# Ranking the weight split of the spilled expert blocks ahead of the list decode in a two-layer encoder step

## The chip, the cores and the metric

The kernel runs on one core of one Trainium2 chip. The metric is device time of one execution in microseconds (us); the kernel before took 3354.44 us, the median of three runs (3349.73 to 3357.75). Engines are named as in the profile: PE multiplies matrices, PEld loads its weights, DVE is the vector engine, ACT the activation engine, POOL the general-purpose one, SP the queue that issues most transfers.

## What is computed

The reference is one step of a two-layer encoder on 512 prompt rows and 32 sample rows of 1024 channels. Each layer has a mixer (attention beside a state-space model, or pooling beside latent attention), an output projection, and a PEER channel mixer: every row picks 16 of 16384 experts for each of 8 heads and sums what they return. The change touches the PEER part alone:

```python
q = (xb @ w_q).reshape(blk, PEER_HEADS, 2, D_HALF)
s = jnp.einsum('nhpd,hpkd->nhpk', q, sub_keys)
sv, si = lax.top_k(s, PEER_TOPK)
cand = sv[:, :, 0, :, None] + sv[:, :, 1, None, :]
cv, ci = lax.top_k(cand.reshape(blk, PEER_HEADS, 256), PEER_TOPK)
eid = i1 * N_KEYS + i2          # i1, i2: si gathered by ci
g = jax.nn.softmax(cv, axis=-1)
act = gelu(einsum('nd,nhkd->nhk', xb, u_tab[eid]))
return einsum('nhk,nhkd->nd', g * act, v_tab[eid])
```

## The kernel before

For rows 128 to 543 (ND = 416) the kernel does not gather experts. It computes all 16384 activations, in 128 blocks of 128 experts, multiplies them by a matrix G that is zero where a row did not choose the expert, and multiplies by the second weights. Rows 0 to 127 are done by gathers (`gather`, L258 and after) that run beside the dense part.

In each layer `peer` runs these stages:

- **List decode** (`topk`, from L285): queries, then for five tiles of rows the scores, the two lists of 16, their 50 candidate sums, the top 16 of these, and the decoding of expert numbers. Nearly all of it is small work on DVE (L279 to L283 are the top-16 steps); two products per tile are on POOL (`W`, L353, and `M`, L364).
- **G build** (`gbuild`, from L394): one-hot tiles on DVE, small matmuls on PE, evictions on ACT (L419), 13 writes of G to DRAM.
- **Spilled blocks** (L170 to L174): the first NSPILL = 80 blocks' activations do not need G. For each, `upass` multiplies the block's first weights with the rows, ACT applies gelu (L173) and SP writes the result to DRAM (`AC`, L174).
- **Dense part** (from L181): the other 48 blocks, and the second product of all 128.

Matrix products are made of fp32 halves: `load_split` (L126) loads a 128x1024 tile `raw`, ACT rounds it to the high part `uh` (L132), DVE subtracts to get the low part `ul` (L133), and a block is 8 x 3 matmuls with 416 columns (L145). There are three buffers for `raw` and two for each of `uh` and `ul`, so the high part of block b can be written only when the matmuls of block b-2 are done.

The program order of each engine is not the order of the source. A scheduler places instructions by rank (the position in the source, unless `tc.high_priority` gives another) among those that it holds to be ready, so the matmuls of spilled blocks, which come last in the source of the three stages, are put into the gaps that the list decode and the G build leave. What the engine runs is then fixed: each works through its own list in order.

Of the kernel before, what the change touches and what calls it, by code (L numbers as in the profile page):

```python
# [41 lines left out]
class Ker:  # L42
# [105 lines left out]
    def peer(s, layer):  # L148
        nc, tc, I = s.nc, s.tc, s.I
        G = s.dram.tile([ND // 32, 128, 128, 32], F32, name='G')  # L150
        AC = s.dram.tile([NSPILL, 128, ND], F32, name='AC')
        with ExitStack() as sc:
# [15 lines left out]
            with ExitStack() as gs:  # L168
                s.gbuild(gs, I1T, I2T, GhT, GlT, G)
            for b in range(NSPILL):  # L170
                ps, = s.upass(I['peer_uT'][layer, b])
                a_ = s.ac.tile([128, ND], F32, name='act')
                nc.scalar.activation(a_, ps[:, :ND], AF.Gelu)  # L173
                nc.sync.dma_start(AC[b], a_)  # L174
# [110 lines left out]
    def topk(s, tk, layer, I1T, I2T, GhT, GlT):  # L285
        nc, tc, I = s.nc, s.tc, s.I
# [5 lines left out]
        for h in range(8):  # L292
            pss = s.upass(I['peer_wq'][layer, h], None, CH)
            for i, (a, c) in enumerate(CH):
                nc.scalar.activation(qT[:, h, a:c], pss[i][:, :c - a], AF.Copy)
        pend = []
        for t, (t0, n) in enumerate(TILES):
            H = 8 if t < 4 else 2
# [1187 lines left out]
```

## Time and profile before

| what | value |
|---|---|
| median of three runs | 3354.44 us |
| the profiled execution | 3355.85 us, of which the span is 3354.1 us |
| PE busy | 3123.9 us (93%) |
| DVE busy | 2665.7 us (79%) |
| ACT busy | 1245.7 us (37%) |
| list decode, layer 0 and layer 1 | 398 to 606 us, 2030 to 2238 us |
| G build | 606 to 778 us, 2238 to 2410 us |
| spilled blocks left after it | 778 to 892 us, 2410 to 2524 us |
| dense part | 892 to about 1680 us, 2524 us to the end |

Busy PE counts pipelined matmuls, so a full row says that matmuls are in flight and not that they start as fast as they can. Idle time before an instruction is put down to the instruction that ended last among those that it waited for.

### The profile page before, as it was taken

The page shows a single profiled execution, that of the slowest core. Times are in us where ns is not written, and L with a number is a line of the kernel's source. Part 1 is how long each engine was busy: PE and PEld are TensorE (multiplying, and loading weights), DVE is VectorE, ACT ScalarE, POOL GpSimd, SP SyncE. Part 2 cuts the span into 40 slices and gives each one's busy share as a digit, 9 for nine tenths or more (in the row PEclk, how much of TensorE's full clock was granted, in tenths as well). Part 3 has the DMA queues.
Part 4 walks back from the last instruction along what each step waited for, and adds up shares of the span by engine and source line. Part 5 has one row for each costly group of instructions (what it writes and reads, how often), then busy time and mean ns, then how long its engine had stood idle before and what let it go on. Part 6 is the DMA issues. An engine that isn't in the chain of part 4 may idle for free.

```text
span 3354.1 us, 48383 instructions
## 1 busy us (share of the span) xinstructions
PE 3123.9 (93%) x17932; PEld 2960.0 (88%) x17932; DVE 2665.7 (79%) x5685; ACT 1245.7 (37%) x2215; POOL 644.0 (19%) x436
## 2 busy tenths in 40 slices
PE   5779967999999999999999998789999999999998
PEld 5667967999999999999988688689999999999998
DVE  7976599993398898888974638999627989899888
ACT  3243323453333333333344423245433333333333
POOL 4443011100021222222210410120001222222221
PEclk8889988999999999999999999899999999999999
DMA  3113223677599999999952132257847999999996
GB/s 119 52 33 115 85 87 115 250 269 245 174 344 334 326 338 350 343 330 340 344 174 67 51 117 90 98 172 278 294 162 263 345 337 346 327 342 343 338 337 248
DMA packets 328265, 781.56 MB, mean 233 GB/s; under 512 B 24318, under 2 KB 178142, under 8 KB 291676
## 3 DMA queue, kind: packets, MB, share of 16 engines
q1 hardware_dynamic: 291164, 510.01, 45.1%
q0 software_dynamic: 36864, 268.45, 20.6%
q8 instruction: 141, 2.31, 0.3%
q14 instruction: 96, 0.79, 0.1%
HBM read 677.65 MB, written 100.73 MB: 232 GB/s over the span
## 4 chain that ended last, share of the span: by engine, by line
PE 48%; issue 22%; DVE 20%; DMA 7%; ACT 2%; POOL 1%; SPq 0%; POOLq 0%; ACTq 0%; DVEq 0%
PE psa L145 12%; PE psb L215 12%; PE psc L215 6%; PE psa L215 6%; DMA raw<-in_peer_uv 4%; PE psa L1012 3%; DVE ul L133 2%; DVE wl L133 1%; DMA uv<-in_peer_uv,eid 1%; DMA act<-AC 1%; DVE trep L281 1%; DVE accg L274 1%; DVE junk L268 1%; DVE X L280 1%; DVE X L283 1%
## 5 line engine op out<-in xcount | busy, mean ns | idle before, releaser
L145 PE MATMUL psa<-hh,ul 128*128 128x416 f32 (+1 forms) x2304 | 807.9, 355 | 87.7 <-DVE ul L133 87.7
L145 PE MATMUL psa<-hh,uh 128*128 128x416 f32 (+1 forms) x2304 | 805.3, 353 | 8.5 <-ACT uh L132 8.4
L145 PE MATMUL psa<-hl,uh 128*128 128x416 f32 (+1 forms) x2304 | 798.9, 350 | 0.0
L265 POOL DMA_INDIRECT uv<-in_peer_uv,eid x256 | 376.5, 1471 | 1770.5 <-DVE accg L274 1673.5
L133 DVE TENSOR_TENSOR ul<-raw,uh 128x1024 fp32r<-128x1024 f32 x268 | 345.3, 1290 | 278.4 <-ACT uh L132 278.2
L145 PEld LDWEIGHTS psa<-hh,ul 128*128 128x128 f32 x2304 | 440.1, 192 | 102.8 <-DVE ul L133 98.4
L132 ACT ACTIVATE uh<-raw 128x1024 fp32r<-128x1024 f32 x272 | 287.5, 1058 | 599.8 <-PE psa L145 510.4
L145 PEld LDWEIGHTS psa<-hh,uh 128*128 128x128 f32 x2304 | 440.7, 193 | 17.5 <-ACT uh L132 12.2
L145 PEld LDWEIGHTS psa<-hl,uh 128*128 128x128 f32 x2304 | 440.3, 193 | 6.0
L132 ACT ACTIVATE wh<-raw 128x1024 fp32r<-128x1024 f32 (+1 forms) x303 | 314.9, 1047 | 229.4 <-DMA raw<-in_peer_uv 165.3
L133 DVE TENSOR_TENSOR wl<-raw,wh 128x1024 fp32r<-128x1024 f32 (+1 forms) x281 | 342.5, 1222 | 55.3 <-ACT wh L132 54.6
L215 PE MATMUL psb<-wh 128*128 128x416 f32 x1024 | 358.1, 353 | 7.2 <-ACT wh L132 7.2
L215 PE MATMUL psb<-wh,wl 128*128 128x416 f32 x1024 | 359.4, 352 | 3.2 <-DVE wl L133 3.1
L215 PE MATMUL psb<-wl,wh 128*128 128x416 f32 x1024 | 357.9, 350 | 0.0
L274 DVE SCALAR_TENSOR_TENSOR accg<-uv,gw,accg 128x1024 f32<-128x1024 f32 x256 | 327.9, 1281 | 3.0
L268 DVE SCALAR_TENSOR_TENSOR junk<-uv,xg 128x1024 f16<-128x1024 f32 x256 | 312.0, 1219 | 21.4 <-DMA uv<-in_peer_uv,eid 21.0
L271 ACT ACTIVATE gw<-gact 128x1 f32<-128x1 f32 x256 | 50.7, 199 | 468.0 <-DVE junk L268 466.8
L196 ACT ACTIVATE wh<-act 128x416 fp32r<-128x416 f32 x256 | 139.2, 549 | 228.0 <-DVE act L194 126.6
L215 PEld LDWEIGHTS psb<-wh 128*128 128x128 f32 x1024 | 192.6, 188 | 11.1 <-ACT wh L132 9.3
L215 PEld LDWEIGHTS psb<-wh,wl 128*128 128x128 f32 x1024 | 192.5, 188 | 7.6 <-DVE wl L133 5.3
L215 PEld LDWEIGHTS psb<-wl,wh 128*128 128x128 f32 x1024 | 192.9, 188 | 1.8
L215 PE MATMUL psc<-wh 128*128 128x416 f32 x512 | 180.1, 352 | 4.9 <-ACT wh L132 4.9
(548 smaller groups left out, 5722.6 us busy)
## 6 DMA issues: line engine op xcount, KB each, us to landing
raw<-in_peer_uT SPq DMA_DIRECT2D x256, 512.0 KB, 4.4
raw<-in_peer_uv SPq DMA_DIRECT2D x256, 512.0 KB, 7.1
G<-st SPq DMA_DIRECT2D x26, 2048.0 KB, 7.3
gt<-G SPq DMA_DIRECT2D x64, 832.0 KB, 11.1
AC<-act SPq DMA_DIRECT2D x160, 208.0 KB, 2.0
act<-AC SPq DMA_DIRECT2D x160, 208.0 KB, 8.8
raw<-in_w_out SPq DMA_DIRECT2D x16, 512.0 KB, 3.3
raw<-in_peer_wq SPq DMA_DIRECT2D x16, 512.0 KB, 3.3
```

Of the source, the lines that this page charges most:

```text
L132: nc.scalar.activation(hi, raw, AF.Copy)
L133: (eng or nc.vector).tensor_sub(lo, raw, hi)
L145: nc.tensor.matmul(pss[i][:, :c - a], w[:, k, :], x[:, k, a:c], start=(k == 0 and j == 0), stop=(k == 7 and j == 2))
L196: nc.scalar.activation(wh, a_, AF.Copy)
L215: nc.tensor.matmul(ps[:, :ND], w[:, d % 4 * 128:(d % 4 + 1) * 128], x, start=(first and q == 0 and j == 0), stop=(last and q == GB - 1 and ...
L265: nc.gpsimd.indirect_dma_start(out=uv, out_offset=None, in_=s.I['peer_uv'].rearrange('l e d -> (l e) d'), in_offset=bass.IndirectOffsetOnA ...
L268: nc.vector.scalar_tensor_tensor(junk, uv[:, 0:1024], 1.0, s.xg, op0=ALU.mult, op1=ALU.mult, accum_out=act[:, i:i + 1])
L271: nc.scalar.activation(w, act, AF.Gelu)
L274: nc.vector.scalar_tensor_tensor(s.accg, rows[i][:, 1024:2048], w[:, i:i + 1], s.accg, op0=ALU.mult, op1=ALU.add)
L280: nc.vector.max_index(idx[:, 0:8], val[:, 0:8], src)
L281: nc.vector.match_replace(out=w[:n], in_to_replace=val[:, 0:8], in_values=src, imm_value=-3e38)
L1012: nc.tensor.matmul(ps[:n, :], l, ww, start=(k == 0 and i == 0), stop=(k == 7 and i == 2))
```

## The change

Per spilled block, `load_split` is called explicitly, under a rank as of the point in the source where the queries are done and the list decode begins (`s.early`); `upass` then takes the finished pair from `s.pre`. The load, the high part and the low part thus rank ahead of the list decode and the G build; the matmuls, the gelu and the write keep their rank.

```diff
@@ -168,6 +168,8 @@
             for b in range(NSPILL):
+                with tc.high_priority(tc.cur_priority - s.early):
+                    s.pre.append(s.load_split(s.up, I['peer_uT'][layer, b], 'u'))
                 ps, = s.upass(I['peer_uT'][layer, b])
@@ -293,6 +295,7 @@
                 nc.scalar.activation(qT[:, h, a:c], pss[i][:, :c - a], AF.Copy)
+        s.early = tc.cur_priority
         pend = []
```

The order of instructions shows what the scheduler made of it. Lines of the changed kernel are two or three higher than those of before from L171 on (L279 to L283 of before are L281 to L285). Rows of each list stand in program order; "x4" is four equal ones in a row.

DVE in the list decode of layer 0, second tile of rows, before: two low parts one behind the other, with none in the 53 rows ahead of them and the 42 behind.

```order
L280 MAX_INDEX X<-V,S 128x8
L281 MATCH_REPLACE trep_3585<-cv,C 128x50
L280 MAX_INDEX X<-V,S 128x8
L279 MAX V<-S 128x8 x3
L133 TENSOR_TENSOR ul<-raw,uh 128x1024 x2
L283 MAX_INDEX X<-V,trep_3688 128x8
L283 MAX_INDEX X<-V,trep_3694 128x8
L282 MAX cv<-trep_3579 128x8
```

The same place in the changed kernel:

```order
L282 MAX_INDEX X<-V,S 128x8 x4
L133 TENSOR_TENSOR ul<-raw,uh 128x1024
L282 MAX_INDEX X<-V,S 128x8 x2
L284 MAX V<-trep_3688 128x8
L284 MAX V<-trep_3694 128x8
L283 MATCH_REPLACE trep_3579<-cv,C 128x50
L282 MAX_INDEX X<-V,S 128x8
L283 MATCH_REPLACE trep_3585<-cv,C 128x50
L282 MAX_INDEX X<-V,S 128x8 x3
L281 MAX V<-S 128x8 x3
L133 TENSOR_TENSOR ul<-raw,uh 128x1024
L285 MAX_INDEX X<-V,trep_3694 128x8
```

The low parts now stand singly, some ten to twenty rows apart. From the first top-16 step to the last instruction of the list decode DVE has 41 of them in each layer (33 before, both counted with the few that belong to the queries).

DVE at the end of the G build of layer 0, before:

```order
L410 TENSOR_TENSOR A<-A,glt 128x1024
L409 TENSOR_TENSOR Ah<-A,ght 128x1024
L133 TENSOR_TENSOR ul<-raw,uh 128x1024
L410 TENSOR_TENSOR A<-A,glt 128x1024
L133 TENSOR_TENSOR ul<-raw,uh 128x1024 x27
L194 TENSOR_TENSOR act<-act,gt 128x416
```

and in the changed kernel:

```order
L410 TENSOR_TENSOR B<-iota_83,i2t 128x1024
L413 TENSOR_TENSOR A<-A,glt 128x1024
L412 TENSOR_TENSOR Ah<-A,ght 128x1024
L413 TENSOR_TENSOR A<-A,glt 128x1024
L133 TENSOR_TENSOR ul<-raw,uh 128x1024 x19
L196 TENSOR_TENSOR act<-act,gt 128x416
```

Of the low parts left after the G build, 27 became 19, in both layers; the G build holds 25 in both kernels. On PE the matmuls of 25.1 blocks stood behind the last one of the G build and now 17.0; ahead of its first one stood 31.1 blocks and now 40.0.

DVE around the second product of a tile (`M`, L363, which POOL multiplies at L364), before:

```order
L363 TENSOR_TENSOR M<-r_3642,rep_85 128x2048
L279 MAX cv<-C 128x8 x3
L345 TENSOR_TENSOR X_3838<-X_3838,starts 128x128
L282 MAX V<-trep_3887 128x8
L279 MAX V<-S 128x8 x2
L282 MAX V<-trep_3893 128x8
```

and in the changed kernel:

```order
L366 TENSOR_TENSOR M<-r_3642,rep_85 128x2048
L281 MAX V<-S 128x8 x2
L284 MAX V<-trep_3893 128x8
L133 TENSOR_TENSOR ul<-raw,uh 128x1024
L282 MAX_INDEX cx<-cv,C 128x8
```

A low part now stands three maxima behind the instruction that lets POOL's product start, where a 128x128 addition stood before.

## Rows read from the trace of the kernel before

**Rows 1.** Busy time: three stages of layer 0, list decode of layer 1.

```profile
core 0: us, PE busy (x) PEld busy (x) DVE busy (x) ACT busy (x) POOL busy (x), PEclk, DMA share, GB/s
398.00:606.00 208.00, 161.22 (x774) 150.89 (x774) 202.43 (x932) 65.16 (x97) 33.26 (x10) 0.89 0.31 103
606.00:778.00 172.00, 171.63 (x1462) 157.96 (x1461) 157.36 (x238) 93.23 (x169) 7.80 (x4) 1.00 0.76 277
778.00:892.00 114.00, 114.00 (x605) 112.96 (x604) 31.42 (x26) 37.18 (x52) 0.00 (x0) 1.00 0.57 196
2030.00:2238.00 208.00, 164.95 (x780) 154.31 (x779) 201.08 (x933) 68.86 (x101) 32.39 (x10) 0.88 0.31 103
```

**Rows 2.** Waits in the list decode of layer 0 (398 to 606 us).

```profile
ACT uh L132 <- PE psa L145: 92.8, 18, 18.7
PE psa L145 <- DVE ul L133: 44.3, 11, 11.7
DVE ul L133 <- ACT uh L132: 7.1, 4, 4.2
```

**Rows 3.** Waits in the list decode of layer 1 (2030 to 2238 us).

```profile
PE psa L145 <- DVE ul L133: 40.6, 11, 12.4
DVE ul L133 <- ACT uh L132: 9.5, 5, 4.2
```

**Rows 4.** Timeline, layer 0 (start, duration, engine, line): two low parts in a row.

```profile
432.55 2.33 DVE L133 TENSOR_TENSOR ul<-raw,uh 128x1024 fp32r<-128x1024 f32 x2
...
433.80 0.72 PE L145 MATMUL psa<-hh,ul 128*128 128x416 f32 x1 [6.59 <-DVE ul L133]
...
435.35 0.55 PE L145 MATMUL psa<-hh,uh 128*128 128x416 f32 x1
...
435.70 0.55 PE L145 MATMUL psa<-hl,uh 128*128 128x416 f32 x1
...
439.00 0.35 PE L145 MATMUL psa<-hh,ul 128*128 128x416 f32 x1
...
439.19 0.35 PE L145 MATMUL psa<-hh,uh 128*128 128x416 f32 x1
```

**Rows 5.** Gelu of spilled blocks by stage: ns min/median/max, first and last start.

```profile
L173 ACT ACTIVATE act<-psa x28: 497/500/539, 411.5 to 601.3; 128x416 f32<-128x416 f32 x28
L173 ACT ACTIVATE act<-psa x26: 500/502/522, 778.0 to 891.1; 128x416 f32<-128x416 f32 x26
L173 ACT ACTIVATE act<-psa x26: 500/502/522, 2409.6 to 2522.7; 128x416 f32<-128x416 f32 x26
```

**Rows 6.** The low part in the list decode of layer 0: min/median/max ns.

```profile
L133 DVE TENSOR_TENSOR ul<-raw,uh x29: 1194/1211/4667, 397.8 to 601.4; 128x1024 fp32r<-128x1024 f32 x29
```

**Rows 7.** DVE groups, same stretch, by shape: busy us, mean ns, idle before.

```profile
L133 DVE TENSOR_TENSOR ul<-raw,uh 128x1024 fp32r<-128x1024 f32 x29 | 41.8, 1447 | 7.1 <-ACT uh L132 7.1
L337 DVE TENSOR_SCALAR z<-z 128x8 f32<-128x8 f32 x4 | 5.4, 1350 | 0.0
L345 DVE TENSOR_TENSOR X<-X,starts 128x128 f32<-128x128 f32 x4 | 4.4, 1103 | 0.0
L342 DVE CAST X<-X 128x128 f16<-128x128 uint32 x4 | 4.2, 1052 | 0.0
L347 DVE COPY D<-X 128x8 f32<-128x8 f32 x4 | 3.4, 858 | 0.0
L336 DVE RECIPROCAL z<-z 128x8 f32<-128x8 f32 x4 | 0.7, 181 | 0.0
```

**Rows 8.** Timeline: a low part that started just behind a product on POOL.

```profile
444.73 3.67 POOL L353 TENSOR_TENSOR W<-M,D 128x2048 f32<-128x2048 f16 x1 [100.90 <-DVE trep L281]
444.87 4.61 DVE L133 TENSOR_TENSOR ul<-raw,uh 128x1024 fp32r<-128x1024 f32 x1
```

**Rows 9.** Product that needs G, reads of G: first and last start.

```profile
L194 DVE TENSOR_TENSOR act<-act,gt x256: 576/584/594, 896.9 to 3307.2; 128x416 f32<-128x416 f32 x128
L185 SPq DMA_DIRECT2D gt<-G x64: 359/371/1781, 784.1 to 3284.1; - x64
```

## The prediction, made before the changed kernel ran

> **What bounds the kernel now.** I read busy time by stage first. In the list decode DVE is busy for 202.4 of 208 us and sets the stage's length, while PE is busy for 161.2 with only 774 matmuls, at a mean granted clock of 0.89 [rows 1]. In the last stretch, where only spilled blocks are left, it is the other way: PE is busy for all of 114 us, DVE for 31.4 [rows 1]. So the same kind of work, spilled blocks, is short of weights in one stage and all that is left in the other. The waits say what it lacks: in the list decode PE stood 44.3 us in layer 0 and 40.6 in layer 1 for the low part of the weights, in 11 waits each [rows 2, 3]. The gelu rows count blocks by stage: 28 start in the list decode, 26 in the stretch after the G build [rows 5]. What the reader should see in the timeline is one such wait: PE stands for 6.59 us until DVE, which had other work first in its list, makes two low parts in a row; then the first matmuls start 0.35 us apart (435.35 and 435.70), and later 0.19 us apart (439.00 and 439.19) [rows 4]. That is the lower of the clock's two levels after idleness, 1.2 against 2.4 GHz, and it explains the 0.89.
>
> **What the change does, part by part.** No instruction of the mathematics is added. In each layer DVE makes 41 low parts where it made 33 before the list decode ends, 25 in the G build as before, and 19 instead of 27 afterwards, as the order in the section on the change shows. So 8 blocks per layer move from the last stretch into the list decode.
>
> *Gain at the end.* There 26 gelus start between 778.0 and 891.1 us, 25 steps of 4.52 us; layer 1 has 2409.6 to 2522.7, again 4.52 [rows 5]. PE is full there and nothing else is, so each block taken away saves a step: 8 x 4.52 = 36.2 us per layer.
>
> *Eight more low parts on DVE in the list decode.* The median one takes 1.211 us [rows 6], and since DVE has 5.6 us free in 208, nothing hides them: 8 x 1.21 = +9.7 us. This is the price of the move.
>
> *What follows a product on POOL.* A low part that started 0.14 us behind a product on POOL took 4.61 us instead of 1.21, ending when the product (3.67 us) had ended and its own work was done [rows 8]. The mean of the 29 is 1.447 [rows 7], so such waits cost 29 x (1.447 - 1.211) = 6.8 us of the stage. In the changed order a low part stands close behind more of the ten products of a tile loop. But DVE is held up there already: four small groups of at most 128 columns average 0.86 to 1.35 us, where one of that kind that is not held up takes 0.18 [rows 7]; their 16 instructions take 17.4 us, some 14 more than their own work. So of the 33.3 us that POOL is busy [rows 1] DVE loses at least 6.8 + 14 = 21 already, and at most 12 are left to lose. I take +2: a low part mostly takes the place of another instruction that would have been held up.
>
> The Trainium skill, page "SBUF — State Buffer", section "Who interferes with whom", says that a DVE instruction with two inputs in SBUF and a GpSimd instruction that reads SBUF exclude each other for a whole instruction. Here the low part is such an instruction and the row of 4.61 us agrees; by that rule taken for each new low part alone the change would come out slower, which is the third rival below.
>
> *DVE waiting for the high part.* With two buffers, ACT can write the high part of a block only when PE is done with the block two before. Before, DVE stood 7.1 us for it over 29 low parts, 9.5 in layer 1, the longest wait 4.2 [rows 2, 3]. What is queued behind a waiting low part is the list decode itself. With 41 low parts at the same mean it would be 7.1 x 41/33 = 8.8, so +1.7 (+2.3 in layer 1). They also stand closer: 208 + 10 us over 41 is 5.3 us each, against a step of 4.52 for PE at full pace. I take +4. The lower end is 0; the upper end, if every one of the 41 waited as the four that did, 41 x 1.8 = 73, is far away, and the row it is nearest to is the 7.1.
>
> *PE in the list decode.* It has 208 - 161.2 = 46.8 us idle [rows 1], the stage grows by 16, and 8 blocks need 36.2. It fits with some 26 us to spare, so PE does not become the bound; a better clock is worth nothing there by itself.
>
> *ACT, SP, DMA.* ACT gets 8 high parts of about 1.1 us and 8 gelus of 0.5, 13 us, in a stage where it is busy for 65 of 208; SP issues 8 more loads and 8 more writes where the DMA engines are busy for 0.31 of the time [rows 1]. Nothing. If that cover went, the load would be late for ACT, and the low part with it.
>
> *G build.* 25 low parts there in both kernels; DVE is busy for 157 of 172 us and PE for all of it [rows 1]. PE has 23.0 blocks there instead of 23.8, at best 0.8 x 4.52 = 3.6 us less. I take 0, since the number on DVE is unchanged.
>
> *Reads of G.* They start at 784.1 us and the first product needs them at 896.9 [rows 9]; with a last stretch of some 78 instead of 114 us they still lie beside it. Nothing. The dense part has the same order and only starts earlier.
>
> **The sum.** Per layer -36.2 + 9.7 + 2 + 4 = -20.5 us, for two layers -41. The profiled execution took 3355.85 us and would take 3314.9; the median shown is 1.4 lower, so I forecast 3313 us. The ends: with low parts at 1.2, no further wait and the 3.6 us of the G build, -36.2 + 9.6 - 3.6 = -30.2 per layer, 3294 us. With all 12 us of POOL lost and three times the wait, -36.2 + 9.7 + 12 + 12 = -2.5 per layer, 3349 us.
>
> **Rivals.**
>
> 1. *PE paces the list decode.* Before, 774 matmuls took 161.2 us of busy PE, 0.208 each, not the 0.188 of a step of 4.52 over 24. At that pace 774 + 8 x 24 = 966 take 201 us out of about 222, and the irregular spacing of the low parts lets PE and DVE wait for each other in turns. For: the clock of 0.89. Against: it is low because of the long waits, which the change shortens. At 14 us of DVE waits instead of 4 the layer gains 10.5, the kernel 21: 3333 us.
>
> 2. *DVE stands before the low parts.* The new wait takes the place of the old one, now on the engine that sets the stage. Its place is the subtraction on L133 behind the high part on L132; it decides from the point at which the 41 low parts wait for (36.2 - 9.7 - 2) / 41 = 0.6 us each on average, 24.5 us per layer. At 1.0 us each, 41 us, the kernel is 33 us slower: 3387. For: the order is fixed by the scheduler's idea of PE's pace, and PE waits are the largest cause of ACT's idleness (92.8 us before the high part [rows 2]). Against: 7.1 us in 29 before.
>
> 3. *Every new low part stands behind a product on POOL.* 8 x (4.61 - 1.21) = 27.2 us instead of 2 per layer: -36.2 + 9.7 + 27.2 + 4 = +4.7, 3364 us. Against it: only ten products per layer, and at most 12 us that DVE does not lose already.
>
> 4. *It does not do what it says.* The order shows the eight blocks moved; but if the stretch after the G build were limited by the reads of G or the writes of activations, shortening it would give nothing: about 3354 + 20, with the price still paid. PE's 114 of 114 us speak against it.
>
> **Chances.** The forecast with its own spread (3294 to 3325) 0.65, rival 1 (3325 to 3347) 0.23, rival 2 0.07, rival 3 0.03, rival 4 0.02. A measurement can tell about 0.2%, 6.7 us, from no change: faster is below 3347.7. Rival 1's last part and a little of the others give 0.05 for no change; of rivals 2 to 4 some 0.07 is slower; faster 0.88. The range of 8 in 10 is 3292 to 3338: the forecast's own spread and the nearer half of rival 1.
>
> **What would show it.** In the profile of the changed kernel: the list decode of each layer longer by 12 to 20 us with DVE still at 97%; some 36 gelus in it instead of 28; PE's wait for the low part, 44.3 and 40.6 us, down to a third; a clock nearer to 1; 17 or 18 gelus 4.52 us apart after the G build. DVE's wait for the high part in that stage above 25 us would prove the forecast wrong by rival 2, a mean low part of over 2 us by rival 3.

## The result, and the profile after

The changed kernel takes 3297.32 us (median of 4 runs, 3294.18 to 3299.37) against 3352.09 us for the kernel before (4 runs, 3346.80 to 3357.75): a ratio of 0.9837, 95% interval 0.9825 to 0.9849. That is 54.8 us faster. The forecast was 41 us, to 3313, in a range of 3292 to 3338. The medians and ratios leave out one execution, a slow one of experiment 2 that took 11032.74 us.

The page of the changed kernel first. Its profiled execution took 3299.37 us, 56.5 less than that of the kernel before.

```profile
span 3297.6 us, 48396 instructions
PE 3119.0 (95%) x17932; PEld 2950.5 (89%) x17932; DVE 2660.7 (81%) x5685; ACT 1246.6 (38%) x2217; POOL 643.4 (20%) x436
```

The same number of matmuls (17932) and of DVE instructions (5685) is done as before; what differs is when. The busy time by stage, cut where the stages now end, answers to [rows 1] (list decode, G build and the rest of layer 0, then the list decode of layer 1; columns: busy us and instructions of PE, its weight loads, DVE, ACT and POOL, then PE's granted clock, DMA share and GB/s).

```profile
399.00:614.00 215.00, 193.32 (x975) 184.38 (x975) 209.17 (x941) 79.61 (x115) 33.62 (x10) 0.96 0.38 128
614.00:786.00 172.00, 171.40 (x1454) 154.93 (x1453) 157.47 (x238) 92.49 (x168) 4.81 (x4) 1.00 0.75 276
786.00:863.00 77.00, 77.00 (x409) 76.29 (x408) 20.00 (x17) 24.91 (x34) 0.00 (x0) 1.00 0.63 212
2005.00:2220.00 215.00, 193.55 (x982) 184.55 (x982) 210.93 (x941) 80.04 (x116) 33.57 (x10) 0.97 0.38 128
```

PE does 975 matmuls in the list decode instead of 774, at a mean granted clock of 0.96 instead of 0.89, and the last stretch is 77 us instead of 114. DVE is still busy for 97% of the list decode. The waits there (layer 0; engine and line that waits, what for, us in total, times, longest) answer to [rows 2]:

```profile
ACT uh L132 <- PE psa L145: 101.8, 25, 8.0
PE psa L145 <- DVE ul L133: 21.7, 11, 3.1
DVE ul L133 <- ACT uh L132: 7.8, 3, 4.2
```

PE's wait for low parts fell from 44.3 to 21.7 us, its longest from 11.7 to 3.1. In layer 1 [rows 3] it fell from 40.6 to 21.5. Of DVE's waits for the high part one of 4.2 us, in each row of either kernel, ends just before the stage begins (at 397.79 us before, at 398.56 now); what happened in the stage itself is taken up below. The gelus of the spilled blocks by stage (min, median, max ns; first and last start) answer to [rows 5], the low part's line to [rows 6]:

```profile
L175 ACT ACTIVATE act<-psa x37: 493/500/540, 412.2 to 612.0; 128x416 f32<-128x416 f32 x37
L175 ACT ACTIVATE act<-psa x17: 498/500/502, 790.0 to 862.5; 128x416 f32<-128x416 f32 x17
L175 ACT ACTIVATE act<-psa x17: 502/502/502, 2394.9 to 2467.5; 128x416 f32<-128x416 f32 x17
...
L133 DVE TENSOR_TENSOR ul<-raw,uh x38: 1195/1206/4545, 398.6 to 612.1; 128x1024 fp32r<-128x1024 f32 x38
```

The 17 gelus after the G build stand (862.5 - 790.0) / 16 = 4.53 us apart, the same step as before: PE's pace there has not changed, there is less to do.

To add up a layer exactly I use four marks: the end of the queries' last eviction, the first one-hot on DVE (the G build begins), the last eviction of the G build, and the last gelu. The two lines that give the inner marks, of the changed kernel:

```profile
L408 DVE TENSOR_TENSOR A<-iota,i1t x52: 680/684/694, 616.3 to 777.3; 128x1024 f16<-128x1024 f16 x52
...
L422 ACT ACTIVATE st<-psb x63: 580/599/668, 631.1 to 785.4; 128x512 f32<-128x512 f32 x63
```

Between these marks (us, layer 0 / layer 1; "gelus" is the count of layer 0 in the three stages by the same marks, which lie a little later than the cuts of [rows 5]):

| kernel | list decode | G build | rest | layer | gelus |
|---|---|---|---|---|---|
| before | 209.5 / 208.4 | 169.3 | 114.4 | 493.3 / 492.1 | 29, 25, 26 |
| changed | 217.2 / 215.7 | 169.7 | 77.0 | 463.9 / 462.5 | 37, 26, 17 |

The list decode holds eight gelus more. The last stretch holds nine fewer and the G build one more, because a block that lies across the border now ends on its other side.

So each layer pays 7.7 or 7.3 us in the list decode and 0.4 in the G build, and gets 37.4 back at the end: 29.4 and 29.6 us less, 59.0 for two layers. The profile as a whole is 56.5 shorter; some 2.5 us are given back outside these stages.

### The profile page after: what moved, and what is told of

It is laid out like the page before. It is cut to its first block, busy times and chain, and to the rows that moved or that the text cites. A ratio compares the mean times of both kernels' runs of the same rounds, so it can differ in the third digit from the quotient of the medians.

```text
span 3297.6 us, 48396 instructions
## 1 busy us (share of the span) xinstructions
PE 3119.0 (95%) x17932; PEld 2950.5 (89%) x17932; DVE 2660.7 (81%) x5685; ACT 1246.6 (38%) x2217; POOL 643.4 (20%) x436
## 4 chain that ended last, share of the span: by engine, by line
PE 59%; DVE 20%; issue 12%; DMA 6%; ACT 2%; POOL 1%; SPq 0%; POOLq 0%; ACTq 0%; DVEq 0%
PE psa L145 20%; PE psb L217 13%; PE psc L217 7%; PE psa L217 7%; DVE ul L133 3%; DMA raw<-in_peer_uv 3%; PE psa L1015 3%; DMA uv<-in_peer_uv,eid 1%; DVE trep L283 1%; DVE wl L133 1%; DVE X L282 1%; DVE X L285 1%; PE psa L1207 1%; DVE accg L276 1%; DVE junk L270 1%
## 5 line engine op out<-in xcount | busy, mean ns | idle before, releaser
L133 DVE TENSOR_TENSOR ul<-raw,uh 128x1024 fp32r<-128x1024 f32 x268 | 358.9, 1339 | 220.5 <-ACT uh L132 220.0
L217 PE MATMUL psb<-wh 128*128 128x416 f32 x1024 | 357.9, 353 | 7.1 <-ACT wh L132 7.1
L217 PE MATMUL psb<-wh,wl 128*128 128x416 f32 x1024 | 359.3, 352 | 3.4 <-DVE wl L133 3.0
L217 PE MATMUL psb<-wl,wh 128*128 128x416 f32 x1024 | 357.7, 350 | 0.0
L270 DVE SCALAR_TENSOR_TENSOR junk<-uv,xg 128x1024 f16<-128x1024 f32 x256 | 312.0, 1219 | 22.6 <-DMA uv<-in_peer_uv,eid 22.3
L217 PEld LDWEIGHTS psb<-wh 128*128 128x128 f32 x1024 | 192.3, 188 | 10.9 <-ACT wh L132 9.2
L217 PEld LDWEIGHTS psb<-wh,wl 128*128 128x128 f32 x1024 | 192.3, 188 | 8.5 <-DVE wl L133 6.2
L217 PEld LDWEIGHTS psb<-wl,wh 128*128 128x128 f32 x1024 | 192.6, 188 | 1.7
L217 PE MATMUL psc<-wh,wl 128*128 128x416 f32 x512 | 180.2, 352 | 2.7 <-DVE wl L133 2.7
```

The costliest lines, as they stand in the source:

```text
L133: (eng or nc.vector).tensor_sub(lo, raw, hi)
L217: nc.tensor.matmul(ps[:, :ND], w[:, d % 4 * 128:(d % 4 + 1) * 128], x, start=(first and q == 0 and j == 0), stop=(last and q == GB - 1 and ...
L270: nc.vector.scalar_tensor_tensor(junk, uv[:, 0:1024], 1.0, s.xg, op0=ALU.mult, op1=ALU.mult, accum_out=act[:, i:i + 1])
```

## The experiments

All edits are to the changed kernel, but for one that says otherwise. Each ratio is to the kernel before, timed on the same chip. Differences in us between two edited kernels go by their medians, though the experiments ran on three chips, on which the kernel before took 3349.01, 3350.85 and 3353.11 us; where this matters the difference by the ratios is given beside it.

**1 and 2. Which of the three ranked steps does it?** The change ranks the load, the high part (ACT) and the low part (DVE) early. If DVE's list is what counts, the rank of the subtraction alone must do.

```diff
+                lo, hi, raw = ...
+                nc.sync.dma_start(raw, I['peer_uT'][layer, b])
+                nc.scalar.activation(hi, raw, AF.Copy)
                 with tc.high_priority(tc.cur_priority - s.early):
-                    s.pre.append(s.load_split(s.up, I['peer_uT'][layer, b], 'u'))
+                    nc.vector.tensor_sub(lo, raw, hi)
+                s.pre.append((hi, lo))
```

> Only the low part (the subtraction on DVE) has the early rank; the load and the high part keep theirs. Theory: what PE lacked in the list decode was DVE's subtraction, so this part alone moves the eight blocks per layer (DVE's list again has 41, 25 and 19 low parts in the three stages) and gives the whole gain: 3297 us, within 6. Rival, that the weights had to be loaded and rounded sooner: little of the gain, 3335 us or more.

Measured: 3298.37 us (3294.86 to 3300.54), ratio 0.9838 (0.9819 to 0.9857). The opposite, with load and high part inside the block and the subtraction outside:

> Only the load and the high part have the early rank; the subtraction on DVE keeps its own. Theory: nothing moves that counts (33, 25 and 27 low parts on DVE as in the kernel before), so 3352 us, within 7. Rival, that the weights had to be loaded and rounded sooner: most of the gain, 3315 us or less.

Measured: 3352.55 us (nine runs, 3346.33 to 3359.25) against 3350.85, ratio 1.0003 (0.9992 to 1.0015). The waits in the list decode of these two kernels, the one of the low part alone first:

```profile
PE psa L145 <- DVE ul L177: 21.7, 12, 3.1
```

and the one of load and high part alone:

```profile
PE psa L145 <- DVE ul L177: 42.8, 11, 12.5
```

The whole gain comes from the place of one instruction per block in DVE's list. With the high part ranked early and the low part not, 29 blocks are done in the list decode, as before, and the layer takes 490.9 us by the marks above; with the low part alone it is 37 blocks and 462.6 us.

**3 and 4. Which blocks?** By the order, 41 low parts are made before the list decode ends. So the rank of the later blocks should be worth nothing.

```diff
-                with tc.high_priority(tc.cur_priority - s.early):
-                    s.pre.append(...)
+                if b < 40:
+                    with tc.high_priority(tc.cur_priority - s.early):
+                        s.pre.append(...)
```

> Only blocks 0 to 39 of each layer have the early rank. Theory: these forty are the ones that lie in the list decode, and in the G build the rank decides nothing, so the whole gain stays: 3297 us, within 6. Rival, that the rank ahead of the G build gives part of it: 3310 us or more.

Measured: 3301.73 us (2 runs), ratio 0.985 (0.9824 to 0.9876). And with `if b >= 40`:

> Only blocks 40 to 79 of each layer have the early rank. Theory: no block moves out of the last stretch (33, 25 and 27 low parts on DVE), so no gain: 3352 us, within 7. Rival, that the rank ahead of the G build gives part of the gain: 3340 us or less.

Measured: 3351.78 us, ratio 0.9994 (0.9983 to 1.0004). The first 40 blocks of a layer carry all of it, within the intervals. With 1 and 2 this closes the rival that the change works by something other than more low parts in the list decode.

**5 and 6. What is a product on POOL worth in DVE's time?** Both products of a tile loop (W and M) move from POOL to DVE.

```diff
-            nc.gpsimd.tensor_tensor(W, M, D[...].to_broadcast(sh), op=ALU.mult)
+            nc.vector.tensor_tensor(W, M, D[...].to_broadcast(sh), op=ALU.mult)
...
-            nc.gpsimd.tensor_tensor(M, M, X2[...].to_broadcast(sh), op=ALU.mult)
+            nc.vector.tensor_tensor(M, M, X2[...].to_broadcast(sh), op=ALU.mult)
```

> The changed kernel with the two products of each tile (W and M of the list decode) on DVE instead of POOL. Theory: each product on POOL holds DVE up for nearly its own length, some 3 us, whichever instruction comes next, so about 25 us per layer; on DVE the two products of a tile should take about 2.2 and 1.2 us, some 14 us per layer. DVE's list holds 46, 24 and 15 low parts, four fewer in the last stretch. So the three stages together get shorter by about 10 us per layer, 3277 us, between 3265 and 3290, and no low part in the list decode takes over 2 us. Rival, that DVE loses only what the low parts show above their median: the products then cost DVE about as much as they free, 3297 us or more.

Measured: 3245.38 us (3241.81 to 3249.24), ratio 0.9691 (0.9675 to 0.9707): 51.9 us below the changed kernel (49 by the ratios), far better than expected. The same edit to the kernel before:

> The kernel before with the two products of each tile on DVE. Theory: the loss of DVE to POOL's products was there before the change too, about 21 to 25 us per layer, so this gains about as much as in the changed kernel, some 10 us per layer plus what four low parts fewer in the last stretch make (38, 24 and 23): 3325 us, between 3310 and 3340. Rival, that only the new low parts suffer from the products: nothing, 3350 us or more.

Measured: 3309.06 us, ratio 0.9877 (0.9861 to 0.9894), a little better than its range and 40.0 us below the kernel before in the same series (3349.01). The two edits do not stand in each other's way: moving the products is worth some 50 us with the change and 40 without. In the profiles both layers together get 50.4 us shorter with the change and 48.2 without it, where the list decode then holds 34 gelus instead of 29; that the two edits help each other is not shown.

My expectation for the first had an error of kind, not of size. I had counted the time that DVE gets free as a shorter list decode, and named the four blocks fewer in the last stretch without their price, 4 x 4.52 = 18.1 us per layer. Stretches of list decode and rest, then the waits there, of the changed kernel with the products on DVE:

```profile
398.00:612.00 214.00, 210.04 (x1103) 201.39 (x1102) 211.38 (x957) 87.03 (x127) 0.18 (x1) 1.00 0.45 146
781.00:836.00 55.00, 55.00 (x295) 54.56 (x294) 15.13 (x13) 18.44 (x26) 0.00 (x0) 1.00 0.70 231
```

```profile
PE psa L145 <- DVE ul L133: 3.7, 7, 1.6
```

The list decode between the marks is 213.9 us, only 3.3 shorter than in the changed kernel. What DVE got free went into five more low parts (42 gelus in the stage instead of 37), and of these blocks four fewer are left for the last stretch and one fewer for the G build: 55.8 us instead of 77.0, and 168.4 instead of 169.7. Layer: 438.1 instead of 463.9. The groups of DVE in the list decode (busy us, mean ns, idle before) show what was bought:

```profile
L133 DVE TENSOR_TENSOR ul<-raw,uh 128x1024 fp32r<-128x1024 f32 x43 | 51.9, 1208 | 4.9 <-ACT uh L132 4.9
...
L356 DVE TENSOR_TENSOR W<-M,D 128x2048 f32<-128x2048 f16 x4 | 9.1, 2278 | 0.0
L367 DVE TENSOR_TENSOR M<-M,X 128x2048 f16<-128x2048 f16 x4 | 9.1, 2276 | 0.0
...
L354 DVE TENSOR_TENSOR M<-pos,rep 128x2048 f16<-128x2048 f16 x4 | 4.8, 1204 | 0.0
```

DVE now does the products itself: 18.2 us for the eight of these rows and 1.4 for the two of the small fifth tile. In return not one of the 43 low parts is held up (mean 1208 ns, where it was 1614 for 38, 15.4 us in all), the smaller instructions that were held up in the changed kernel are back at their own length (6.4 us in all), and DVE's waits for ACT and POOL fell from 9.0 to 4.9 (each with the 4.2 that end before the stage). So 25.9 us came free for 19.6, some 6 us, and the five more low parts took 6.0 of them. Those five blocks, 4.52 us each, are 22.6 of the 25.8 us that the layer gained. Of the 3.3 us by which the list decode is shorter, 1.4 are a shorter wait of DVE for PE at its end (2.8 to 1.4 us before the first one-hot); the rest is not accounted for. PE waits 3.7 us in all for low parts and has a granted clock of 1.00.

**7. Would the low part be better on POOL?** POOL is busy for 34 of 215 us in the list decode and DVE is full.

```diff
-                    s.pre.append(s.load_split(s.up, I['peer_uT'][layer, b], 'u'))
+                    s.pre.append(s.load_split(s.up, I['peer_uT'][layer, b], 'u', nc.gpsimd))
```

> The changed kernel with the low parts of the spilled blocks on POOL instead of DVE. It takes the price of the low parts (1.2 us each on DVE) away from DVE. Theory: on POOL one takes 2.4 us, as in the rows of the queries' weights, and holds DVE up meanwhile when DVE's instruction needs the same access, so the price comes back; the scheduler also puts only 30 blocks ahead of the G build and leaves 32 for the last stretch, 15 more than the changed kernel, at 4.52 us each: slower than the changed kernel, 3340 us or more. Rival, that the low parts on DVE are the only thing that sets the list decode: faster than the changed kernel, 3280 us or less.

Measured: 3448.67 us (2 runs), ratio 1.0294 (1.0266 to 1.0321). The three stages of layer 0, and the low part in the first of them:

```profile
398.00:604.00 206.00, 162.04 (x774) 152.09 (x774) 189.35 (x904) 67.30 (x100) 102.22 (x39) 0.89 0.31 101
604.00:791.00 187.00, 154.16 (x1303) 140.02 (x1302) 149.27 (x212) 83.94 (x156) 105.33 (x24) 0.91 0.61 231
791.00:936.00 145.00, 145.00 (x769) 143.83 (x768) 2.45 (x2) 46.83 (x64) 71.94 (x30) 1.00 0.56 188
```

```profile
L133 POOL TENSOR_TENSOR ul<-raw,uh x29: 2340/2397/3233, 398.2 to 600.8; 128x1024 fp32r<-128x1024 f32 x29
```

and in the G build:

```profile
L133 POOL TENSOR_TENSOR ul<-raw,uh x20: 2339/2720/15282, 609.2 to 787.8; 128x1024 fp32r<-128x1024 f32 x20
```

A low part takes 2.40 us on POOL and 1.21 on DVE, and in the G build, beside DVE's one-hot work, up to 15.28. The list decode has 774 matmuls, as the kernel before; PE now wants for low parts in the G build as well (25.6 us; PE busy for 154 of 187 us, clock 0.91), and 32 blocks are left for the end instead of 17. An idle engine is no gain if the starved engine does not get its input sooner from it. That the length of 2.40 us is the cause in the list decode is not shown: POOL is busy for only 102 of 206 us there and stands 67.2 for high parts. What sets the pace in that stage stays open.

**8 to 10. Is the second buffer of the high part the next limit?** ACT stands 101.8 us for PE before it can write a high part (the first wait line of the changed kernel). A third buffer for it takes SBUF that one of the six activation buffers gives up.

```diff
-ACB = 6
+ACB = 5
...
-        hi = pool.tile([128, 1024], F32R, name=name + "h")[:, :w]
+        hi = pool.tile([128, 1024], F32R, name=name + "h", **({'bufs': 3} if name == 'u' else {}))[:, :w]
```

> The changed kernel with three buffers for the high part instead of two (and five instead of six for the activations, to make room). It takes away most of what DVE and ACT can wait for there: the high part no longer needs the matmuls of two blocks before to be done. Theory: DVE waited only about as long as before in the list decode, so at most those few microseconds per layer come off: 3292 us, between 3284 and 3300. Rival, that DVE now stands before the low parts: 15 us or more per layer come off, 3270 us or less.

Measured: 3282.92 us (3279.78 to 3287.24), ratio 0.9796 (0.9779 to 0.9812). Alone this reads as 14.4 us for a third buffer, more than expected and just below the range. Two things changed, though, so the other half was run by itself (`ACB = 5`, two buffers of the high part):

> The changed kernel with five buffers for the activations instead of six, and nothing else: the control for the run with three buffers for the high part. Theory: the same as the changed kernel, 3297 us, within 6, so that what that run gained is the third buffer's. Rival, that one activation buffer fewer shifts the dense part by itself: 3290 us or less.

Measured: 3288.56 us (3287.31 to 3290.03), ratio 0.981 (0.9788 to 0.9832). I had expected no difference from 3297 within 6; the rival held: 8.8 of the 14.4 us (9.0 by the ratios) come from one activation buffer fewer, and 5.6 (4.7 by the ratios) from the third high part.

The smaller `ACB` does not shorten the stages of the layer: they are 464.1 and 462.5 us, against 463.9 and 462.5. What became shorter lies between the last gelu of layer 0's spilled blocks and the end of layer 1's queries, 1133.0 us instead of 1142.6 (862.5 to 2005.1 in the changed kernel). The ratio's interval overlaps that of the changed kernel at its edge (0.9825 to 0.9849), but the slowest of the four runs, 3290.03, is 4 us below the fastest of the changed kernel. The other traces say more. From the last gelu of the spilled blocks to the last matmul of the second product (L217, in the kernel before L215) the dense part of both layers together takes 1625.7 us with `ACB = 5`, 1626.6 with the third high part as well and 1634.9 in the changed kernel. The three kernels with six buffers that hold 37 gelus in the list decode (the changed one, experiments 1 and 3) take 1633.5 to 1634.9; with the products on DVE it is 1627.5 with six buffers (experiment 5) and 1623.8 with five (the last run below). That one activation buffer fewer shortens the dense part is shown; by which wait is not, and stays open.

For the third high part the intervals overlap, and its 5.6 us stand on the medians. In the profiles its two layers are 6.7 us shorter than with `ACB = 5` alone (919.9 against 926.6), but the whole spans differ by only 1.3 (3285.0 against 3286.3), since 3.1 us are lost between the dense part of layer 0 and the end of layer 1's queries, 1.3 ahead of layer 0's list decode and 0.9 in the dense parts. So it shortens the stages, and what that is worth to the kernel is not settled.

Both together with the products on DVE:

> The changed kernel with the products on DVE and with three buffers for the high part (five for the activations). In the kernel with the products on DVE alone, PE waits for only 3.7 us per layer in the list decode, so the three stages are PE's there. Theory: almost nothing is left to win in them, 0 to 4 us per layer; what else the third buffer gave (some 3 us per layer outside the three stages) comes on top: 3235 us, between 3228 and 3246. Rival, that the two-buffer handshake still costs something everywhere: 3225 us or less.

Measured: 3237.94 us (3235.77 to 3238.79), ratio 0.9659 (0.9638 to 0.9681). It beats both kernels, by 115 and 59 us, and is the best version found. It is 7.4 us below the products on DVE alone (10.7 by the ratios, whose intervals overlap), and the layer by the marks is 437.1 instead of 438.1 us. With the products off POOL the third buffer has little left to do: by the medians and these marks most of the 7.4 lies outside the three stages, as with the smaller `ACB`: the dense part of both layers takes 1623.8 us instead of 1627.5.

## Why the prediction was right, and where its sum was off

The direction, the mechanism and the stage that pays were right; the time lies inside the range, 16 us below the forecast and 5 above its lower end. Term by term (us per layer, layer 0; layer 1):

| term | predicted | measured | how (layer 0) |
|---|---|---|---|
| blocks off the last stretch | -36.2 | -37.4; -37.4 | rest 114.4 to 77.0 |
| low parts on DVE | +9.7 | +9.7; +9.7 | 8 more gelus; 1206 ns median |
| what follows a product on POOL | +2 | -2.9; +0.5 | below |
| DVE waiting for the high part | +4 | -1.5; -3.4 | 5.1 to 3.6 in the stage |
| DVE waiting for PE and POOL at the end of the list decode | none | +3.3; +2.0 | 0.6 to 4.0 |
| G build | 0 | +0.4; +0.4 | 169.3 to 169.7 |

The terms add up to -28.4 and -28.2 us, where the marks give -29.4 and -29.6; the remainder is not accounted for. Both side terms of the list decode were priced too dear, and a wait that the prediction did not have gave a part of it back: one of 2.8 us for PE before the first one-hot (0.4 before) and one of 1.2 for POOL's last product. So the sum came out within 9 us per layer in part by luck.

**The gain at the end** was priced by the one row that could price it, the step of 4.52 us [rows 5]. It held because PE alone set that stretch and still does (77.00 of 77.00 us).

**DVE waiting for the high part** was the term furthest off. I scaled [rows 2] by the number of low parts and then raised it because the low parts would stand closer together. The base was misread: 4.2 of its 7.1 us end before the stage begins, and a wait of 2.2 us for a low part at 606.27 lies behind the end of the rows' window. In the stage by the marks DVE stood 5.1 us in four waits before and 3.6 in two now; in layer 1 it was 5.3 in four and is 1.9 in one. So rival 2 (the new wait on the engine that sets the stage) falls: it decided from 24.5 us, and even the whole row has 7.8. Why the wait fell while the low parts rose from 30 to 38 in the stage stays open. The pairs of [rows 4] are not the reason, for DVE does not wait at either pair; all four waits before lie near the end of the stage, at 569.7, 573.9, 601.4 and 606.3 us.

**The products on POOL** were thought through rightly and still rated too dear. After the change low parts are held up more often, as rival 3 has it: five in the list decode of layer 0, where it was two. The timeline of the changed kernel at one product (start, duration, engine, line):

```profile
468.81 3.64 POOL L367 TENSOR_TENSOR M<-M,X 128x2048 f16<-128x2048 f16 x1 [16.03 <-DVE M L366]
469.25 4.28 DVE L133 TENSOR_TENSOR ul<-raw,uh 128x1024 fp32r<-128x1024 f32 x1
473.58 0.46 PE L145 MATMUL psa<-hh,ul 128*128 128x416 f32 x1 [3.07 <-DVE ul L133]
```

The low part ends 4.28 us after its start, 1.08 us after the product, and PE has stood 3.07 us for it. The same product in the kernel before:

```profile
463.98 3.64 POOL L364 TENSOR_TENSOR M<-M,X 128x2048 f16<-128x2048 f16 x1 [15.59 <-DVE M L363]
...
464.17 3.61 DVE L345 TENSOR_TENSOR X<-X,starts 128x128 f32<-128x128 f32 x1
```

There a 128x128 addition, which takes 0.27 us when nothing is in its way, was held up for 3.61. The groups of DVE in the list decode of the changed kernel add this up (busy us, mean ns):

```profile
L133 DVE TENSOR_TENSOR ul<-raw,uh 128x1024 fp32r<-128x1024 f32 x38 | 61.3, 1614 | 7.8 <-ACT uh L132 7.8
...
L350 DVE COPY D<-X 128x8 f32<-128x8 f32 x4 | 3.3, 816 | 0.0
...
L348 DVE TENSOR_TENSOR X<-X,starts 128x128 f32<-128x128 f32 x4 | 1.1, 270 | 0.0
...
L345 DVE CAST X<-X 128x128 f16<-128x128 uint32 x4 | 0.9, 216 | 0.0
...
L340 DVE TENSOR_SCALAR z<-z 128x8 f32<-128x8 f32 x4 | 0.6, 150 | 0.0
```

The excess of the low parts over their median rose from 6.8 us to 38 x (1.614 - 1.206) = 15.5, so by 8.7. The four small groups of [rows 7] fell: the addition from 4.4 to 1.1 us, the tensor_scalar from 5.4 to 0.6, the cast from 4.2 to 0.9, the copy from 3.4 to 3.3, together by 11.6 (4 instructions each, by the means of [rows 7] and of these rows). Net -2.9 instead of +2. In layer 1 the low parts' excess rose by 4.9 us, from 12.1 to 17.0, and the addition and the copy fell by 4.4: net +0.5. In these two layers a product on POOL takes its toll of DVE about once, from the instruction of this kind that comes next; more low parts in the list change who pays, and the total by little. Rival 3 charged each new low part in full and let nobody else off.

The Trainium skill, page "SBUF — State Buffer", section "Who interferes with whom", has the rule behind rival 3, that a DVE instruction with two inputs in SBUF and a GpSimd (here POOL) instruction that reads SBUF exclude each other for the whole instruction. The rows of 4.28 and 3.61 us agree with it. The groups show beside it that in layer 0 the sum over the stage fell while more of the large instructions were hit.

**Rival 1**, that PE would pace the list decode, is out as well: the 975 matmuls took 193.3 us of 215, 0.198 each instead of the feared 0.208; the longest wait fell from 11.7 to 3.1 us, and the granted clock rose with it from 0.89 to 0.96. DVE still sets the stage at 97%.

**The signs I had named.** Gelus in the stage: 37, forecast 36. Clock: 0.96 and 0.97. 17 gelus 4.53 us apart at the end. Mean low part 1.614 us, under the 2 that would have proved rival 3. The list decode grew by 7.7 and 7.3 us, less than the 12 to 20 named, by the terms above. PE's wait went to a half (21.7 of 44.3), not to a third. Of the 11 waits that are left, five (10.7 us) stand behind a low part that a product on POOL held up, and six (11.0 us) behind low parts of their own length. With the products on DVE all are 3.7 us (experiment 5), but the order of DVE's list changed there too, so how much of this is POOL's doing and how much the scheduler's is not shown.

## What to carry to other kernels

Where one engine starves in a stage and is the only bound of a later one, price the engine that feeds it by exchange: here 1.21 us of DVE in the list decode bought 4.52 us of PE at the end, and DVE time that is freed there turned for the most part into more fed blocks and not into a shorter stage (experiment 5). Before ranking several steps of a producer early, find the one that stands in the full engine's list; here the subtraction alone did all of it. And when a product on a side engine holds up the full one, move the product over and weigh its length there (2.28 us) against what it held up, before moving anything else away from it.

## What the runs showed of the hardware that was not expected

- A product on POOL (3.64 us) holds up even very small DVE instructions: the copy of 8 columns on L350 averages 816 ns in the changed kernel, and 154 with the products on DVE.
- On DVE both products of 2048 columns take 2.28 us, whether the output is f32 (L356, 2278 ns) or f16 (L367, 2276 ns). The f16 comparison of the same size (L354) takes 1.20 us. I had expected about 1.2 for the one with f16 output.
- The subtraction of 1024 columns takes 2.40 us on POOL and 1.21 us on DVE. On POOL beside the G build one took 15.28 us (experiment 7).
- One activation buffer fewer (`ACB` 5 instead of 6) made the kernel 8.8 us faster, outside the stages that the change touches, in the dense part; the cause is open.
